# Attention by couples of heads or maps: three one-pass score products on 64-row tiles, A's values as fp32 on 64-column tiles

## The chip, the cores and the metric

The kernel runs on one NeuronCore of a Trainium2 chip. Its engines are named as in the profile: PE multiplies matrices (PEld is its loading of the stationary operand, the weights), DVE, ACT and POOL do vector work, SP issues the DMAs. The metric is the device time of one execution in microseconds (us), the median of a few runs.

## What is computed

One layer of an encoder for two groups of requests (prompt and sample), each with 1024 positions of 1024 channels, all in fp32. A common input projection feeds two attention branches. Branch A has 8 query heads and 2 key/value heads of 64 channels; branch B has 4 heads, each with two softmax maps of 64 channels, subtracted from each other, and values of 128 channels. Cut to what matters here:

```
# A: qa (S, 8, 64), ka and va (S, 2, 64), after RMSNorm and rotary positions; head j uses key/value head j // 4
s = einsum('bqgrd,bkgd->bgrqk', qblk, k) / sqrt(64)
p = softmax(s, axis=-1)
oa = einsum('bgrqk,bkgd->bqgrd', p, v) * silu(za)
# B: qb and kb (S, 4, 2, 64), vb (S, 4, 128)
s = einsum('bqhmd,bkhmd->bhmqk', qblk, k) / sqrt(64)
p = softmax(s, axis=-1)
pd = p[:, :, 0] - lam * p[:, :, 1]
ob = rms_norm(einsum('bhqk,bkhe->bqhe', pd, v), subln_g) * (1 - lam_init) * silu(zb)
# merge
merged = sigmoid(ga) * (oa @ w_proj_a) + sigmoid(gb) * (ob @ w_proj_b)
y = x + gate * (merged @ w_out)
```

## The kernel before

The two groups are worked on one after the other. A matrix product in full precision is made of one-pass products (type fp32r): each operand is split into a high part, the value rounded to fp32r, and a low part, the rest, and high x high, high x low and low x high are added in PSUM. The projections do that with three products for each block (`proj_tt` at L497 for 128 tokens x 256 columns, `z_gen` at L679, `merge_gen` at L950, `out_gen` at L979). An operand that stays plain fp32 needs no split; PE then takes more passes for one call.

**Scores.** A head has only 64 channels, and the array has 128 rows. `pairs_T` transposes q and k after the rotary step and stacks the high part of 64 channels on 64 partitions and the low part on the other 64: a head's [high; low] fills 128 rows. One product with [high; low] of q and of k gives high x high + low x low; for the cross terms `swapped` makes a copy of q with the halves exchanged, by four DMAs for each two query tiles of two maps (two for one head). So a tile of 128 queries x 1024 keys takes four products of 512 columns (L709, L710) into one score buffer `s` of two PSUM banks. There are two such buffers (`ps_s`).

**Softmax.** DVE takes the maximum of the tile (L711), ACT the exponential with the sum of a row (L712), into a buffer `p` (`ppool`, four of them). `flip` has DVE transpose 32 x 32 blocks in place (L745), for B after the two maps are combined (L744), and four DMAs bring the rows to their partitions in `pT` (L750, `qpool`, two buffers): the transposed weights of 256 queries.

**Values.** For A, `pT_pieces` splits `pT` into high and low in four pieces (ACT at L758, DVE at L759), and `a_values` multiplies a stationary operand that holds the high values of a head in 64 columns and the low ones in the other 64: for each of 8 blocks of keys one product with the high part (L770), one with the low part (L771). The result's two halves of 64 partitions are added at the end (L786, L787). For B the constant `WHOLE` makes the values plain fp32: one call for each block of keys, with 128 columns (L810).

**Order.** `units_of` lists the units of attention: A has 8 heads x 4 pairs of query tiles for each group, B 4 heads x 4. `attention` lays the steps of the units on a time axis: the scores of unit n at n and after, its values from n + `BEHIND`; a flip is issued after the next step. `weave` mixes these steps with the projections by fixed shares. All this only sets priorities: a scheduler with a timeline of its own then fixes the order on each engine, in which attention's steps go ahead (`tc.high_priority`). Engines work strictly in that order and wait for each other by semaphores. SP's queue holds every DMA of the kernel.

The functions concerned:

Of the kernel before, what the change touches and what calls it, by code (L numbers as in the profile page):

```python
# [20 lines left out]
P = 128  # L21
# [43 lines left out]
BEHIND = 1.4  # L65
AHEAD = 100
PV_LAG = 2

WHOLE = (True, True)
# [21 lines left out]
def kernel(ctx: ExitStack, tc: tile.TileContext, t: dict):  # L91
# [8 lines left out]
    qpool = ent(tc.tile_pool(name="qpool", bufs=2))  # L100
    tpool = ent(tc.tile_pool(name="tpool", bufs=2))
# [403 lines left out]
    def rms(ps, nh, e):  # L505
# [3 lines left out]
        nc.scalar.activation(raw, ps, AF.Copy)  # L509
# [31 lines left out]
    def pairs_T(x3, even, odd):  # L541


        nb = x3.shape[1] // 2
        ps = gbank()[:, : nb * P].rearrange("p (b n) -> p b n", b=nb)
        x = x3.rearrange("p (b two) d -> p b (two d)", two=2)
        for b in range(nb):
            nc.tensor.transpose(ps[:, b, :], x[:, b, :], ident)
        for dst, hi, lo in ((even, LO, HI), (odd, HI, LO)):
            nc.scalar.activation(dst[hi], ps[hi], AF.Copy)  # L550
            nc.vector.tensor_tensor(out=dst[lo], in0=ps[hi], in1=dst[hi].bitcast(F32), op=ALU.subtract)
# [15 lines left out]
    def swapped(u):  # L567

        qs = u["q"]
        sw = mtile("sw", [P, 2, 256], F32R)[:, : len(qs)]  # L570
        sl = slice(u["pr"] * 256, u["pr"] * 256 + 256)
        for m, q in enumerate(qs):
            for a, b in ((LO, HI), (HI, LO)):
                dma(sw[a, m].bitcast(F32), q[b, sl].bitcast(F32))
        return sw


    made = {}

# [3 lines left out]
    def kva_gen(ht, out):  # L583
        w = kva_w.pop()[0] if kva_w else load_w(w_cols(w_in, (C_KA, 256)))
        k = v2(utile())
        va = utile().rearrange("p (n k d) -> p n k d", n=NTT, k=2)
        out["ka"], out["va"] = k, va

        def front(tt, ps):
            e = by_turns(tt)  # L590
            x3, s3 = rms(ps[:, :128], 2, e)
            vp = ps[:, 128:256].rearrange("p (k d) -> p k d", k=2)
            vt = va[:, tt]
            nc.scalar.activation(vt[:, :, 0:64], vp, AF.Copy)
            nc.vector.tensor_tensor(out=vt[:, :, 64:128], in0=vp, in1=vt[:, :, 0:64].bitcast(F32), op=ALU.subtract)
            e.tensor_tensor(out=x3, in0=x3, in1=gka.unsqueeze(1).to_broadcast([P, 2, HD]), op=ALU.mult)
            rope(x3, s3, out["cosA"][:, tt], out["sinA"][:, tt], 16, e)
            return x3

        def back(tt, x3):  # L600
            sl = slice(tt * P, (tt + 1) * P)
            pairs_T(x3, k[:, 0:1, sl], k[:, 1:2, sl])
# [3 lines left out]
    def qa_gen(st, half):  # L606
        w = load_w(w_cols(w_in, (C_QA + half * 256, 256)))
# [4 lines left out]
        def front(tt, ps):  # L612
            e = by_turns(tt)
            x3, s3 = rms(ps, 4, e)
# [4 lines left out]
        def back(tt, x3):  # L619
            sl = slice(tt * P, (tt + 1) * P)  # L620
            pairs_T(x3, qs[0][:, :, sl], qs[1][:, :, sl])
            made[id(qs)] = tt + 1
# [3 lines left out]
    def qkb_gen(ht, out, h):  # L626
# [11 lines left out]
        def back(tt, x3):  # L638
            sl = slice(tt * P, (tt + 1) * P)
            pairs_T(x3, qk[0][:, :, sl], qk[1][:, :, sl])  # L640
            made[id(qk)] = tt + 1
# [3 lines left out]
    def vb_gen(ht, out, pr):  # L645
        w = load_w(w_cols(w_in, (C_VB + pr * 256, 256)))
        if WHOLE[pr]:
            v = utile().bitcast(F32).rearrange("p (n h e) -> p n h e", n=NTT, h=2)
            out[2 * pr], out[2 * pr + 1] = v[:, :, 0], v[:, :, 1]
        else:  # L650
            vs = [utile().rearrange("p (n s e) -> p n s e", n=NTT, s=2) for _ in range(2)]
            out[2 * pr], out[2 * pr + 1] = vs
        for tt in range(NTT):
            ps = yield from proj_tt(ht, w, tt)
            if WHOLE[pr]:
                nc.scalar.activation(v[:, tt].rearrange("p h e -> p (h e)"), ps, AF.Copy)
                yield 1
                continue
            for i in range(2):
                vp = ps[:, i * P : (i + 1) * P]  # L660
                nc.scalar.activation(vs[i][:, tt, 0, :], vp, AF.Copy)
                nc.vector.tensor_tensor(
                    out=vs[i][:, tt, 1, :], in0=vp, in1=vs[i][:, tt, 0, :].bitcast(F32), op=ALU.subtract
                )
# [38 lines left out]
    def softmax_unit(q, sw, k, pt, su):  # L703

        m = tiny.tile([P, 1], F32, tag="m", name=nm("m"))
        s = sbank()
        for n in range(2):
            sl = slice(n * 512, (n + 1) * 512)
            nc.tensor.matmul(s[:, sl], q, k[:, sl], start=True, stop=False)  # L709
            nc.tensor.matmul(s[:, sl], sw, k[:, sl], start=False, stop=True)  # L710
        nc.vector.tensor_reduce(out=m, in_=s, axis=AX.X, op=ALU.max, negate=True)  # L711
        nc.scalar.activation(  # L712
            pt.rearrange("p (j c a) -> p j c a", j=4, c=8), s.rearrange("p (c a j) -> p j c a", c=8, j=4),
            AF.Exp, bias=m, accum_out=su,
        )

    def scores(u, i):

        nm_ = len(u["q"])
        t, m = i // nm_, i % nm_  # L720
        qt = u["pr"] * 2 + t
        if "sw" not in u:
            u["sw"] = swapped(u)
        pt = ptile()
        su = u["su"][:, qt : qt + 1] if m == 0 else tiny.tile([P, 1], F32, tag="su", name=nm("su"))
        softmax_unit(u["q"][m][:, qt * P : (qt + 1) * P], u["sw"][:, m, t * P : (t + 1) * P], u["k"][m], pt, su)
        if m == 0:
            u[t] = [pt]
        else:
            f = tiny.tile([P, 1], F32, tag="r", name=nm("r"))  # L730
            nc.vector.reciprocal(f, su)
            nc.gpsimd.tensor_scalar(
                out=f, in0=f, scalar1=u["su"][:, qt : qt + 1], scalar2=nlam, op0=ALU.mult, op1=ALU.mult
            )
            u[t] += [pt, f]
        return t if m == nm_ - 1 else None

    def flip(u, t):


        pt = u[t][0]
        if len(u[t]) > 1:
            _, p1, f = u[t]
            nc.vector.scalar_tensor_tensor(out=pt, in0=p1, scalar=f, in1=pt, op0=ALU.mult, op1=ALU.add)  # L744
        nc.vector.transpose(pt, pt)  # L745
        if t == 0:
            u["pT"] = pair(F32R)
        dst = u["pT"].bitcast(F32).rearrange("p (i t f) -> p i t f", i=4, t=2)
        for i in range(4):
            dma(dst[:, i, t], pt[i * 32 : i * 32 + 32])  # L750

    def pT_pieces(u):

        pT = u["pT"].rearrange("p (q c b) -> p c q b", q=8, c=8)
        for cc in range(4):
            tl = pT[:, cc * 2 : cc * 2 + 2]
            th = tpool.tile([P, 2, 8, 32], F32R, tag="hi", name=nm("hi"), bufs=3)
            nc.scalar.activation(th, tl.bitcast(F32), AF.Copy)  # L758
            nc.vector.tensor_tensor(out=tl, in0=tl.bitcast(F32), in1=th.bitcast(F32), op=ALU.subtract)  # L759
            yield cc, th, tl  # L760

    def a_values(u):
        acc = ps_a.tile([P, 512], F32, tag="a", name=nm("a"))[:, :256]
        ready = []

        def pv(cc, th, tl):
            for c in range(2):
                k = cc * 2 + c
                lt = u["v"](k)
                nc.tensor.matmul(acc, lt, th[:, c, :], start=(k == 0), stop=False)  # L770
                nc.tensor.matmul(acc, lt, tl[:, c, :], start=False, stop=(k == 7))  # L771

        for piece in pT_pieces(u):
            ready.append(piece)
            if len(ready) > PV_LAG:
                pv(*ready.pop(0))
            yield 1
        while len(ready) > 1:
            pv(*ready.pop(0))
            yield 1  # L780
        pv(*ready.pop())
        tmp = mtile("at", [P, 256], bufs=1)
        o = mtile("oo", [P, 256])
        j = u["j"]
        a, b = (slice(0, 64), slice(64, 128)) if j % 2 == 0 else (slice(64, 128), slice(0, 64))
        nc.scalar.activation(tmp[a], acc[b], AF.Copy)  # L786
        nc.vector.tensor_tensor(  # L787
            out=query_order(o[a]), in0=piece_order(acc[a]), in1=piece_order(tmp[a]), op=ALU.add
        )
        pr = u["pr"]  # L790
        dma(u["od"][pr // 2][a, (pr % 2) * 256 : (pr % 2 + 1) * 256], o[a])
        yield 1

    def b_values(u):
        acc = ps_a.tile([P, 512], F32, tag="a", name=nm("a"))[:, :256]
        ready = []
        def pv(cc, th, tl):
            for c in range(2):
                k = cc * 2 + c
                for s, rt in ((0, th), (0, tl), (1, th)):  # L800
                    nc.tensor.matmul(
                        acc, u["v"][:, k, s, :], rt[:, c, :],
                        start=(k == 0 and s == 0 and rt is th), stop=(k == 7 and s == 1),
                    )

        if WHOLE[u["h"] // 2]:
            pT = u["pT"].bitcast(F32).rearrange("p (q c b) -> p c q b", q=8, c=8)
            yield 1
            for k in range(NCH):
                nc.tensor.matmul(acc, u["v"][:, k], pT[:, k], start=(k == 0), stop=(k == 7))  # L810
                if k % 2:
                    yield 1
        else:
            for piece in pT_pieces(u):
                ready.append(piece)
                if len(ready) > PV_LAG:
                    pv(*ready.pop(0))
                yield 1
            while len(ready) > 1:
                pv(*ready.pop(0))  # L820
# [361 lines left out]
```

## Time and profile before

| what | us |
|---|---|
| runs: median (lowest to highest) | 1984.13 (1981.57 to 1989.72) |
| span of the profiled execution | 1985.5 |
| DMA: mean rate over the span | 149 GB/s |
| mean granted TensorE clock | 0.982 of full |

The runs give the time of whole executions; the profile shows one of them instruction by instruction, and its span lies within 0.1% of the median. In the 40 equal slices of the span (49.6 us each) a digit is the busy share in tenths:

```profile
PE   8889999999999998999999899999999999999999
DVE  4558877777877577547465877677788845665641
ACT  4435655665654444754323565556655534566310
PEclk9899999999999999999999999999999999999999
```

PE is near full in every slice but the first; DVE and ACT have room on the mean, though not at every moment.

### The profile page before, as it was taken

Reading aid. Unit: us, or ns where it says so; the run is one execution under the profiler, and the core shown is the slowest. Engines: PE = TensorE matmul, PEld = TensorE weight load, DVE = VectorE, ACT = ScalarE, POOL = GpSimd, SP = SyncE. Lnnn points to the kernel's source line nnn. Section 1 sums busy time; section 2 is a strip of 40 time slices with the busy share of each in tenths; the row PEclk is TensorE's granted clock in tenths of the full one; section 3 lists DMA queues with packets and bytes.
Section 4 is the critical chain, followed back from the end, with each engine's and each line's share of the span. In section 5 each row is a group of like instructions: output and inputs, shape, how many; then the busy total and the mean of one; then the engine's idle time right before and its main releaser. Section 6 shows DMA issues by size and latency. Waiting matters only on the chain.

```text
span 1985.5 us, 30670 instructions
## 1 busy us (share of the span) xinstructions
PE 1908.6 (96%) x10466; PEld 1627.8 (82%) x10466; DVE 1330.8 (67%) x1906; ACT 1009.9 (51%) x1939; POOL 758.1 (38%) x1008
## 2 busy tenths in 40 slices
PE   8889999999999998999999899999999999999999
PEld 3878888888878994778888787888887888877887
DVE  4558877777877577547465877677788845665641
ACT  4435655665654444754323565556655534566310
POOL 2374612453446252221235464134445626422110
PEclk9899999999999999999999999999999999999999
DMA  8124556555553345865641455565654333567532
GB/s 310 33 80 126 155 152 169 152 166 154 133 153 102 101 120 173 257 227 167 222 149 35 140 144 145 149 164 144 184 137 137 106 97 99 156 212 245 174 101 75
DMA packets 269531, 295.11 MB, mean 149 GB/s; under 512 B 35776, under 2 KB 218176, under 8 KB 269376
## 3 DMA queue, kind: packets, MB, share of 16 engines
q1 hardware_dynamic: 269376, 293.15, 49.7%
q8 instruction: 84, 1.38, 0.3%
q14 instruction: 71, 0.58, 0.1%
HBM read 133.59 MB, written 42.01 MB: 88 GB/s over the span
## 4 chain that ended last, share of the span: by engine, by line
PE 68%; DMA 8%; DVE 8%; ACT 5%; SPq 4%; issue 3%; POOL 3%; ACTq 0%; POOLq 0%; DVEq 0%
PE f L497 16%; PE f L679 16%; PE f L950 6%; PE f L979 5%; PE s L709 4%; PE a L810 4%; PE s L710 4%; PE s L979 4%; DMA q<-p 3%; SPq L750 3%; PE s L950 2%; DVE q L759 2%; PE a L771 2%; PE a L770 2%; DVE m L711 2%
## 5 line engine op out<-in xcount | busy, mean ns | idle before, releaser
L679 PE MATMUL f<-u,w 128*128 128x512 f32 x2232 | 582.3, 398 | 0.1
L497 PE MATMUL f<-w,u 128*128 128x256 f32 x3456 | 487.0, 286 | 2.2 <-ACT ev L685 1.4
L497 PEld LDWEIGHTS f<-w,u 128*128 128x128 f32 x3456 | 459.5, 192 | 22.4 <-ACT ev L685 1.8
L679 PEld LDWEIGHTS f<-u,w 128*128 128x128 f32 x2232 | 408.8, 190 | 77.3 <-POOL w L181 0.8
L181 POOL TENSOR_TENSOR w<-st,w 128x512 fp32r<-128x512 f32 x168 | 230.3, 1390 | 439.9 <-ACT w L179 375.1
L712 ACT ACTIVATE p<-s,m 128x1024 f32<-128x1024 f32 x256 | 284.4, 1111 | 206.3 <-DVE m L711 111.3
L711 DVE TENSOR_REDUCE m<-s 128x1 f32<-128x1024 f32 x256 | 310.0, 1216 | 51.3 <-PE s L710 48.7
L745 DVE STREAM_TRANSPOSE p<-p 128x1024 f32<-128x1024 f32 x192 | 238.2, 1241 | 99.2 <-ACT p L712 86.5
L759 DVE TENSOR_TENSOR q<-q,hi 128x512 fp32r<-128x512 f32 x256 | 198.3, 792 | 60.6 <-ACT hi L758 58.6
L515 POOL TENSOR_TENSOR rs<-ss,nhalf 128x4 f32<-128x4 f32 (+1 forms) x112 | 112.8, 1007 | 322.8 <-DVE ss L514 284.0
L758 ACT ACTIVATE hi<-q 128x512 fp32r<-128x512 f32 x256 | 153.8, 625 | 104.1 <-DMA q<-p 55.4
L710 PE MATMUL s<-u,sw 128*128 128x512 f32 x512 | 206.7, 404 | 0.0
L179 ACT ACTIVATE w<-st 128x512 fp32r<-128x512 f32 x196 | 113.9, 625 | 97.2 <-DMA st<-in_w_in_dram 46.0
L950 PE MATMUL f<-u,w 128*128 128x512 f32 x552 | 133.4, 395 | 5.1 <-ACT ev L685 4.4
L770 PE MATMUL a<-hi,u 128*128 128x256 f32 x512 | 132.5, 285 | 2.1 <-DVE oo L787 2.1
L771 PE MATMUL a<-q,u 128*128 128x256 f32 x512 | 129.8, 286 | 1.2 <-DVE q L759 1.2
L810 PE MATMUL a<-q,u 128*128 128x256 f32 x512 | 128.3, 390 | 1.9 <-DVE oo L826 1.5
L950 PEld LDWEIGHTS f<-u,w 128*128 128x128 f32 x552 | 103.9, 190 | 27.2 <-ACT ev L685 4.7
L709 PE MATMUL s<-u 128*128 128x512 f32 x256 | 110.9, 433 | 15.1 <-ACT p L712 15.1
L810 PEld LDWEIGHTS a<-q,u 128*128 128x128 f32 x512 | 97.8, 196 | 17.5 <-DVE oo L826 1.6
L709 PE MATMUL s<-u,u 128*128 128x512 f32 x256 | 103.6, 405 | 8.3 <-ACT p L712 7.7
L710 PEld LDWEIGHTS s<-u,sw 128*128 128x128 f32 x512 | 98.4, 192 | 15.5
(175 smaller groups left out, 2562.1 us busy)
## 6 DMA issues: line engine op xcount, KB each, us to landing
q<-p SPq DMA_DIRECT2D x768, 128.0 KB, 2.6
st<-in_w_in_dram SPq DMA_DIRECT2D x132, 256.0 KB, 3.0
zd<-ev SPq DMA_DIRECT2D x96, 256.0 KB, 2.2
sw<-u SPq DMA_DIRECT2D x256, 64.0 KB, 2.1
p<-zd SPq DMA_DIRECT2D x64, 256.0 KB, 3.2
u<-in_w_ada_dram SPq DMA_DIRECT2D x8, 1024.0 KB, 10.4
st<-in_w_in_dram SPq DMA_DIRECT2D x64, 128.0 KB, 2.7
st<-in_w_out_dram SPq DMA_DIRECT2D x32, 256.0 KB, 2.9
```

The source lines that it names most:

```text
L181: e.tensor_tensor(out=wl, in0=st, in1=wh.bitcast(F32), op=ALU.subtract)
L497: nc.tensor.matmul(ps, lt[c][:, sl], w[:, c, wi, :], start=(k == 0), stop=(k == 23))
L679: nc.tensor.matmul(ps, w[:, c, wi, e * P : (e + 1) * P], rt[c], start=(k == 0), stop=(k == 23),)
L709: nc.tensor.matmul(s[:, sl], q, k[:, sl], start=True, stop=False)
L710: nc.tensor.matmul(s[:, sl], sw, k[:, sl], start=False, stop=True)
L711: nc.vector.tensor_reduce(out=m, in_=s, axis=AX.X, op=ALU.max, negate=True)
L712: nc.scalar.activation(pt.rearrange("p (j c a) -> p j c a", j=4, c=8), s.rearrange("p (c a j) -> p j c a", c=8, j=4), AF.Exp, bias=m, accu ...
L745: nc.vector.transpose(pt, pt)
L759: nc.vector.tensor_tensor(out=tl, in0=tl.bitcast(F32), in1=th.bitcast(F32), op=ALU.subtract)
L810: nc.tensor.matmul(acc, u["v"][:, k], pT[:, k], start=(k == 0), stop=(k == 7))
L950: nc.tensor.matmul(ps, w[:, c, wi, d * P : (d + 1) * P], o[:, oi, :], start=(k == 0), stop=(k == 11))
L979: nc.tensor.matmul(ps, w[:, c, wi, e * P : (e + 1) * P], m[:, mi, :], start=(k == 0), stop=(k == 23))
```

## The change

Attention works on **couples**: for A the heads j and j + 4, which use different key/value heads; for B the two maps of a head.

- **q and k.** `split_T` replaces `pairs_T`: the transposed tile of two heads (128 partitions, 64 for each) is split into a high tile and a low tile, by one ACT and one DVE instruction on 128 partitions instead of two each on 64. `swapped` and its DMAs go. `qa_gen` loads two pieces of 128 columns so that a couple's heads lie together, and `rms` crosses them (`crossed=True`).
- **Scores.** `scores` makes a group for one query tile of a couple: for each half of the keys and each of the three terms high x high, low x high, high x low (`TERMS`) one product for each of the two heads. Each product uses 64 rows of the array, one head the lower 64, the other the upper 64, and the heads alternate: 12 products of 512 columns. Low x low is no longer computed. The group takes both score buffers, and its first product is made to wait for the exponentials of the group before.
- **Values of A.** No split: `va` and `pT` are plain fp32. A unit is a couple, and each call of `a_values` uses 64 columns of the array and writes 64 partitions of the accumulator; the heads alternate: 16 calls of 256 columns. One ACT instruction copies the result. `qpool` has three buffers, and a unit of A takes two.
- **Order.** `together` binds a group: its first product is placed by the scheduler as before, each following one is tied behind the one before it and gets the highest priority. A's units are half as many, each with two steps of scores and two of values (`PAIRS`).
- B's values stay as they are. The shares of the projections in `weave` are unchanged.

The diff, cut to its core:

```diff
+PAIRS = (1.3, 0.3)
+TERMS = ((0, 0), (1, 0), (0, 1))
+TOP = 100000
 AHEAD = 100
-PV_LAG = 2
-WHOLE = (True, True)
...
-    qpool = ent(tc.tile_pool(name="qpool", bufs=2))
-    tpool = ent(tc.tile_pool(name="tpool", bufs=2))
+    qpool = ent(tc.tile_pool(name="qpool", bufs=3))
...
-    def pairs_T(x3, even, odd):
+    def split_T(x3, hi, lo):
...
-        for dst, hi, lo in ((even, LO, HI), (odd, HI, LO)):
-            nc.scalar.activation(dst[hi], ps[hi], AF.Copy)
-            nc.vector.tensor_tensor(out=dst[lo], in0=ps[hi], in1=dst[hi].bitcast(F32), op=ALU.subtract)
+        nc.scalar.activation(hi, ps, AF.Copy)
+        nc.vector.tensor_tensor(out=lo, in0=ps, in1=hi.bitcast(F32), op=ALU.subtract)
+    def together(calls, after=()):
+        prev = None
+        for call in calls:
+            if prev is None:
+                ins = call()
+                for other in after:
+                    behind(ins, other, mybir.DependencyClass.Sync)
+            else:
+                with tc.high_priority(offset=TOP):
+                    ins = call()
+                behind(ins, prev, mybir.DependencyClass.NoSync)
+            prev = ins
...
-            nc.tensor.matmul(s[:, sl], q, k[:, sl], start=True, stop=False)
-            nc.tensor.matmul(s[:, sl], sw, k[:, sl], start=False, stop=True)
...
+        ss = [sbank(), sbank()]
+        for n in range(2):
             sl = slice(n * 512, (n + 1) * 512)
+            for i, (a, b) in enumerate(TERMS):
+                for m in (1, 0):
+                    rows = (LO, HI)[m]
+                    calls.append(lambda m=m, a=a, b=b, rows=rows, sl=sl, i=i: nc.tensor.matmul(
+                        ss[m][:, sl], u["q"][a][rows, qs], u["k"][b][rows, sl],
+                        start=(i == 0), stop=(i == len(TERMS) - 1),
+                    ))
+        together(calls, list(exps))
...
     def a_values(u):
         acc = ps_a.tile([P, 512], F32, tag="a", name=nm("a"))[:, :256]
...
+        together([
+            lambda k=k, m=m: nc.tensor.matmul(
+                acc[(LO, HI)[m]], u["v"][:, k, m], pT[m][:, k], start=(k == 0), stop=(k == 7)
+            )
+            for k in range(NCH) for m in (1, 0)
+        ])
+        yield 1
         o = mtile("oo", [P, 256])
+        nc.scalar.activation(query_order(o), piece_order(acc), AF.Copy)
...
-            na, nv = (2, 4 + PV_LAG) if ph < 2 else (4, 5 + PV_LAG)
-            steps += [(n + i / na, ph, n, i, True) for i in range(na)]
-            steps += [(n + BEHIND + i / nv, ph, n, i, False) for i in range(nv)]
+            nv, behind, pace = (2, *PAIRS) if ph < 2 else (7, BEHIND, 1.0)
+            steps += [(n + i / 2, ph, n, i, True) for i in range(2)]
+            steps += [(n + behind + i * pace / nv, ph, n, i, False) for i in range(nv)]
```

How the instructions move is seen in the order in which each engine holds them. On PE, in the first half of A's heads of the first request group, before (`s` is a score buffer, `u` q, k or a part of the input, `sw` the swapped q, `f` a projection's bank, `w` its weights, `a` the accumulator of A's values, `hi` and `q` the two parts of the transposed weights):

```order
L497 MATMUL f_1868<-w_1435,u_283 128x256
L497 MATMUL f_1868<-w_1435,u_284 128x256
L497 MATMUL f_1868<-w_1435,u_283 128x256 x2
L497 MATMUL f_1868<-w_1435,u_284 128x256
L771 MATMUL a_1682<-q_1573,u_397 128x256
L770 MATMUL a_1682<-hi_1730,u_397 128x256
L771 MATMUL a_1682<-q_1573,u_397 128x256
L497 MATMUL f_1868<-w_1435,u_327 128x256 x2
L709 MATMUL s_1956<-u_396,u_927 128x512
L710 MATMUL s_1956<-u_396,sw_1888 128x512
L709 MATMUL s_1956<-u_396,u_927 128x512
L710 MATMUL s_1956<-u_396,sw_1888 128x512
```

The same place now, at the end of one group of scores, with the values of a couple after it and before the next group:

```order
L714 MATMUL s_1925<-u_393,u_904 128x512
L714 MATMUL s_1924<-u_393,u_904 128x512
L668 MATMUL f_2084<-u_324,w_1865 128x512
L668 MATMUL f_2084<-u_325,w_1865 128x512
L668 MATMUL f_2084<-u_324,w_1865 128x512
L496 MATMUL f_2190<-w_1396,u_530 128x256 x2
L496 MATMUL f_2190<-w_1396,u_531 128x256
L496 MATMUL f_2190<-w_1396,u_530 128x256 x2
L496 MATMUL f_2190<-w_1396,u_531 128x256
L496 MATMUL f_2190<-w_1396,u_530 128x256 x2
L496 MATMUL f_2190<-w_1396,u_531 128x256
```

```order
L496 MATMUL f_2190<-w_1396,u_548 128x256
L753 MATMUL a_1974<-q_1805,u_394 64x256
L753 MATMUL a_1974<-q_1804,u_394 64x256
L753 MATMUL a_1974<-q_1805,u_394 64x256
L753 MATMUL a_1974<-q_1804,u_394 64x256
L753 MATMUL a_1974<-q_1805,u_394 64x256
```

Where products of scores and values stood alone among the projections, they stand in closed groups: 12 of scores (122 of the 128 groups exactly so, one more run holds nearly two of them), 16 of values (all 32). Over the whole program PE goes 133 times into a run of scores, 32 times into a run of A's values and 147 times back to other work.

On DVE, in the same phase, before (L711 the maximum, L745 the transposition, L759 the low part of a piece, L787 the addition of the halves):

```order
L711 TENSOR_REDUCE m_2737<-s_2738 128x1
L745 STREAM_TRANSPOSE p_2695<-p_2695 128x1024
L759 TENSOR_TENSOR q_2429<-q_2429,hi_2600 128x2x8x32
L787 TENSOR_TENSOR oo_2575<-a_2465,at_2574 64x4x2x32
L711 TENSOR_REDUCE m_2782<-s_2783 128x1
L745 STREAM_TRANSPOSE p_2736<-p_2736 128x1024
L759 TENSOR_TENSOR q_2429<-q_2429,hi_2625 128x2x8x32
L759 TENSOR_TENSOR q_2552<-q_2552,hi_2692 128x2x8x32
```

and now:

```order
L695 TENSOR_REDUCE m_1908<-s_1892 128x1
L695 TENSOR_REDUCE m_1911<-s_1893 128x1
L744 STREAM_TRANSPOSE p_1906<-p_1906 128x1024
L744 STREAM_TRANSPOSE p_1907<-p_1907 128x1024
L517 TENSOR_REDUCE ss_2135<-row_2132 128x4
L553 TENSOR_TENSOR u_1418<-f_2147,u_1417 128x2x128
L518 TENSOR_SCALAR ss_2135<-ss_2135 128x4
L695 TENSOR_REDUCE m_1940<-s_1924 128x1
L695 TENSOR_REDUCE m_1943<-s_1925 128x1
```

The maxima of a couple and its transpositions now come in twos, and the instructions on pieces are gone.

224 lines of the change are left out of this document (75 added, 149 removed).

## The prediction

> **What bounds the kernel now.** I read the page's engine shares first, then its chain, then the groups, then PE's waits, and last the timeline, to get from instruction to instruction.
>
> ```profile
> PE 1908.6 (96%) x10466; PEld 1627.8 (82%) x10466; DVE 1330.8 (67%) x1906; ACT 1009.9 (51%) x1939; POOL 758.1 (38%) x1008
> PE 68%; DMA 8%; DVE 8%; ACT 5%; SPq 4%; issue 3%; POOL 3%; ACTq 0%; POOLq 0%; DVEq 0%
> ```
>
> PE is idle for 1985.5 - 1908.6 = 76.9 us only, and two thirds of the chain is its own work. So the change is worth what it does to PE's time, and the other engines matter as far as PE waits for them. What PE waits for (waiting line, releaser, us in total, times, longest):
>
> ```profile
> PE s L709 <- ACT p L712: 22.8, 20, 4.0
> PE a L770 <- DVE oo L787: 2.1, 1, 2.1
> PE a L771 <- DVE q L759: 1.2, 2, 0.9
> ```
>
> The groups that the change touches (count | busy us, mean ns of one | idle before):
>
> ```profile
> L709 PE MATMUL s<-u 128*128 128x512 f32 x256 | 110.9, 433 | 15.1 <-ACT p L712 15.1
> L710 PE MATMUL s<-u,sw 128*128 128x512 f32 x512 | 206.7, 404 | 0.0
> L770 PE MATMUL a<-hi,u 128*128 128x256 f32 x512 | 132.5, 285 | 2.1 <-DVE oo L787 2.1
> L771 PE MATMUL a<-q,u 128*128 128x256 f32 x512 | 129.8, 286 | 1.2 <-DVE q L759 1.2
> L759 DVE TENSOR_TENSOR q<-q,hi 128x512 fp32r<-128x512 f32 x256 | 198.3, 792 | 60.6 <-ACT hi L758 58.6
> L758 ACT ACTIVATE hi<-q 128x512 fp32r<-128x512 f32 x256 | 153.8, 625 | 104.1 <-DMA q<-p 55.4
> ```
>
> A mean of 404 ns is not what a product costs, since products overlap; the distance from start to start is. The timeline (start us, us, engine, line):
>
> ```profile
> 508.49 0.28 PE L770 MATMUL a<-hi,u 128*128 128x256 f32 x1
> ...
> 509.80 0.28 PE L771 MATMUL a<-q,u 128*128 128x256 f32 x1
> 509.92 0.29 PE L497 MATMUL f<-w,u 128*128 128x256 f32 x1
> ...
> 512.46 0.40 PE L709 MATMUL s<-u 128*128 128x512 f32 x1
> 512.70 0.39 PE L710 MATMUL s<-u,sw 128*128 128x512 f32 x1
> 512.92 0.40 PE L709 MATMUL s<-u 128*128 128x512 f32 x1
> 513.16 0.39 PE L710 MATMUL s<-u,sw 128*128 128x512 f32 x1
> 513.39 1.07 PE L679 MATMUL f<-u,w 128*128 128x512 f32 x4
> ...
> 568.60 1.46 PE L810 MATMUL a<-q,u 128*128 128x256 f32 x6
> ```
>
> The four score products take 513.39 - 512.46 = 0.93, so **0.231 us** each (512 columns, one pass). The twelve value products ahead of it take 509.92 - 508.49 = 1.43, so **0.119 us** each (256 columns, one pass). An fp32 product of 256 columns is recorded twice (512 records for 256 calls at L810): six records, (1.46 - 0.38) / 5 = **0.216 us** a record, 0.43 a call.
>
> **What is removed.** Scores: 256 tiles x 4 products x 0.231 = 236.5 us. A's values: 64 units x 16 x 0.119 = 121.9. And the first load of a tile is often exposed: L709's mean of 433 against 404 for L710 is 0.029 x 256 = 7.4, call it 8. Together 366 us of PE. Off PE: the splits of the transposed weights (L758, L759), the adding of halves for A, half the instructions of the q/k splits, 256 DMAs for the swapped q.
>
> **What is added on PE, if pairs overlap.** The trace has no two tiles of the array at work together, so the overlap itself is bounded: from two at the price of one (a slot of 0.231 holds both) to none. I take the first: a pair uses different rows or columns of the array and writes different banks, or different partitions of one, and the nearest rows show that PE runs independent work side by side (a load beside a product at 755.55, quoted below). Scores: 128 groups x 6 slots x 0.231 = 177.4. Values: 32 groups of 16 fp32 calls, 32 records; the second record of one map runs beside the first of the other, so 17 slots x 0.216 = 3.67, x 32 = 117.5. Sum 295, which is 71 below what goes.
>
> **What a change of tile shape costs.** This is what eats the 71. The trace has a few such changes, around the products with only two columns of weights (L435):
>
> ```profile
> 753.84 1.45 PE L435 MATMUL f<-st,cT 128*2 128x512 f32 x3
> 755.22 0.19 PEld L709 LDWEIGHTS s<-u 128*128 128x128 f32 x1 [0.86 <-DVE u L551]
> 755.22 0.50 PE L709 MATMUL s<-u 128*128 128x512 f32 x1
> 755.33 0.19 PEld L710 LDWEIGHTS s<-u,sw 128*128 128x128 f32 x1
> 755.55 0.40 PE L710 MATMUL s<-u,sw 128*128 128x512 f32 x1
> 755.56 0.65 PEld L832 LDWEIGHTS f<-ones_c,at 128*128 128x128 f32 x4
> ...
> 773.38 0.40 PE L710 MATMUL s<-u,sw 128*128 128x512 f32 x1
> 773.71 0.59 PE L435 MATMUL f<-st,cT 128*2 128x512 f32 x1
> ```
>
> Into the narrow shape, at 773: from L710 to L435 0.33 instead of 0.23, so 0.10. Out of it, at 755: the three L435 stand (1.45 - 0.59) / 2 = 0.43 apart, the third starts at 754.70, L709 at 755.22: 0.52, so 0.09 more. And the next load is no longer hidden: PEld L709 starts with its product, not a product earlier, and L709 to L710 takes 0.33, again 0.10 more. The loads follow each other at 755.22 and 755.33: a load of 128 columns occupies its path for 0.107.
>
> So, by the order of the changed program, which changes shape 312 times:
> - 133 entries into the 64-row shape: 0.10 + 0.107 for the first load, + 0.107 until the other half is loaded = 0.31; 41 us.
> - 32 entries into the 64-column shape: 0.10 + 0.05 (half the columns); 5 us.
> - 147 returns to the whole array: 0.09 + 0.10; 28 us.
>
> 74 in all; the rows bound it from 0 (each change falls where PE waits anyway) to 74. I take it whole, since PE rarely waits. Products and changes: 295 + 74 - 366 = **+3 us**. The new products are worth nothing by themselves.
>
> **What is won off PE.** The splits were 198.3 of DVE's 1330.8 and 153.8 of ACT's 1009.9: 15% of each, and some smaller pieces go with them. PE's 76.9 us of idle time lie partly in the first 140 us, which the change hardly touches:
>
> ```profile
> 0.00:60.00 60.00, 52.34 (x192) 25.82 (x193) 26.40 (x48) 24.46 (x41) 12.57 (x16) 0.89 0.79 274
> 60.00:140.00 80.00, 69.52 (x468) 64.29 (x467) 50.93 (x130) 36.01 (x98) 43.81 (x62) 0.95 0.14 44
> ```
>
> 7.7 + 10.5 = 18 there (the second number is the stretch, the third PE busy), 59 after. Bounds: nothing, to some 45 of them. I take a quarter, 15: the waits for L787 and L759 vanish and the one for L712 shrinks. On SP's queue the 256 swap DMAs go and 16 weight loads come (q's columns in two pieces). One wait stays there:
>
> ```profile
> SPq L750 <- PE a L771: 88.1, 40, 6.1
> ```
>
> A's transposed weights wait for the values of the unit before to free their buffer, and the weight loads queue behind. With three buffers and two taken by a unit it waits as before; PE's projections, whose weights lie a tile ahead, hide it, and uncovered it could cost its 88 at most.
>
> Sum against the profiled execution: 1985.5 + 3 - 15 = 1973.5; that execution lies 1.4 above the median of the runs, so **1972 us**.
>
> **The new wait.** A group takes both score banks, so its first product waits for both exponentials of the group before. Queued behind it are the projections on PE, whose banks ACT and DVE wait for. The softmax of a group:
>
> ```profile
> L711 DVE TENSOR_REDUCE m<-s 128x1 f32<-128x1024 f32 x256 | 310.0, 1216 | 51.3 <-PE s L710 48.7
> L712 ACT ACTIVATE p<-s,m 128x1024 f32<-128x1024 f32 x256 | 284.4, 1111 | 206.3 <-DVE m L711 111.3
> ...
> 515.00 1.23 DVE L711 TENSOR_REDUCE m<-s 128x1 f32<-128x1024 f32 x1
> 520.47 1.12 ACT L712 ACTIVATE p<-s,m 128x1024 f32<-128x1024 f32 x1 [0.89 <-DMA q<-p]
> ...
> busy tenths in 40 slices 0002222212232223200000222222123321230000
> ```
>
> With free engines that is 2 x 1.22 + 1.11 = 3.5, and some tenths for the last drain. PE's other work between groups: exponentials run in 28 of the 40 slices of 49.6 us (last row), 1390 / 128 = 10.9 a group, less 1.9 for the group, 9.0 (by the order and the rows above half the gaps are under 7.6). So 3.5 fits well; but the tile of 512.46 ended at 513.55 and its exponential at 521.59, 8.0 later, through queues. I cost the wait at nothing beyond today's 22.8, because those queues held the splits.
>
> **The rivals.**
> - **Half a pair.** The load of a 64-row tile cannot run while the product in the same rows does. For it speaks that an exposed load is just what the changes of shape show; against it that within one shape loads run beside products (755.56 above). A slot is then 0.231 + 0.107; 768 x 0.107 = +82: about **2054**. The Trainium skill states it so (TensorE: Matmul & The Clock Gate, part 3, The mechanism): a weight load overlaps a running matmul only when the row groups differ; the whole-array rows here do not agree. By the speedups measured on that page for four row tiles, 3.07, the estimate would be a slot of 0.30 and some 2025.
> - **No pair at all**, the change does not do what it says: values alone +15 slots x 0.216 x 32 = +104, **2076**; scores too, +177, **2253**. Nothing in the trace speaks for or against.
> - **The bank wait decides** (slower). If queues stay as at 512, a group's chain is 8.0 + 2.3 for the second reduction and exponential = 10.3, over 9.0 by 1.3: in the 64 groups of A +83, **2055**. It decides once the chain passes the work between groups. For it: SP and the weight tiles still hold exponentials up (the row of 520.47 waits for a DMA). Against: DVE and ACT lose 15% or more.
> - **More relief** (faster): idle falls by 45, and the second half's load runs beside the first's (-14): **1928**.
>
> **How the numbers follow.** The forecast, with its own range 1950 to 1995, 0.48; half a pair 0.12; no pair 0.12; bank wait 0.13; relief 0.15. What lies within 0.5% (1974 to 1994) a measurement of this kernel cannot tell from no change. Faster: 0.25 of the forecast's 0.48, and relief's 0.15: 0.40. Same: 0.18. Slower: 0.05 of the forecast's, and 0.37 of the three rivals: 0.42. The range leaves out "no pair" and the ends of the others: 1915 to 2070.
>
> **What would show it.** In the profile after: the two products of a pair start within about 0.11 and the next pair 0.23 later (0.34: half a pair; every product 0.23 after the last: none). The first whole-array product behind a group has its load start with it. PE's waits have a row of the scores for L695's and L698's work, its total near 20 (over 60: the bank wait). DVE falls under 1130 busy and ACT under 860. I am wrong if PE's own time, without waits, moves by over 20 us either way.

## The result, and the profile after

The changed kernel takes 2004.47 us (median of 4 runs, 2002.37 to 2009.5) against 1984.2 before: a ratio of 1.0109, 95% interval 1.0083 to 1.0135. The forecast was 1972. The time lies in the stated range, but on the other side of the kernel before. The profile below shows the slowest of the four runs (2009.5).

The page of the changed kernel: span, engine shares, and PE's and the clock's digits over 40 slices.

```profile
span 2007.7 us, 30209 instructions
PE 1900.4 (95%) x10978; PEld 1525.8 (76%) x10978; DVE 1052.5 (52%) x1458; ACT 819.8 (41%) x1547; POOL 710.8 (35%) x1008
PE   8889999999998998799999899999999899987999
PEclk9899999999999999899999899999999999988999
PE 73%; DMA 8%; DVE 5%; ACT 4%; issue 4%; POOL 3%; SPq 3%; ACTq 0%; POOLq 0%; DVEq 0%
```

DVE lost 278 us of work and ACT 190, PE 8 of busy time. But PE's idle time rose, from 76.9 to 107.3, and the clock falls below full in more slices.

One group of scores in the timeline of PE, with the loads (PEld) beside it:

```profile
501.27 1.08 PE L668 MATMUL f<-u,w 128*128 128x512 f32 x4
502.28 0.50 PE L714 MATMUL s<-u 64*128 64x512 f32 x2
502.62 0.62 PE L714 MATMUL s<-u,u 64*128 64x512 f32 x4
503.08 0.40 PE L714 MATMUL s<-u 64*128 64x512 f32 x2
503.31 0.63 PE L714 MATMUL s<-u,u 64*128 64x512 f32 x4
503.87 0.50 PE L496 MATMUL f<-w,u 128*128 128x256 f32 x2
...
502.28 0.18 PEld L714 LDWEIGHTS s<-u 64*128 64x128 f32 x2 [0.36 <-issue]
502.39 0.42 PEld L714 LDWEIGHTS s<-u,u 64*128 64x128 f32 x4
503.87 0.42 PEld L496 LDWEIGHTS f<-w,u 128*128 128x128 f32 x3 [0.36 <-issue]
```

Two products stand under 502.28 and last 0.50 together: the pair starts at once. The next pair comes 0.34 later, its first load not being hidden; from 502.62 to 503.08 two pairs take 0.46, so a slot is 0.23. The loads come in twos as well: two of 128 columns under 502.28 and the next at 502.39. The last L668 starts at 501.27 + 3 x 0.23 = 501.96, so entering costs 0.32 - 0.23 = 0.09; the first product behind the group again has its load with it. From 502.28 to 503.87 are 1.59, with 0.09 ahead and 0.10 for the load behind **1.78** a group, against 8 x 0.231 = 1.85 for the two tiles before. A group of A's values, and the row of all of them:

```profile
1308.92 3.87 PE L753 MATMUL a<-q,u 128*64 128x256 f32 x32 [0.94 <-DMA q<-p]
1312.72 0.72 PE L668 MATMUL f<-u,w 128*128 128x512 f32 x2
...
L753 PE MATMUL a<-q,u 128*64 128x256 f32 x1024 | 119.6, 385 | 4.8 <-DMA zd<-ev 3.1
```

1312.72 - 1308.92 = 3.80 with its changes of shape, against 32 x 0.119 = 3.81 before. So PE's work itself fell a little: 128 x 0.07 = 9 us.

**Where the time is lost.** I cut both executions at the first score and the last value of each stretch, and in each took from its length the work of PE: products counted, times their cost from rows such as these (0.227, 0.120, 0.216 for an fp32 record, 0.231 for a score before; 1.78 and 3.81 for the new groups with their changes of shape). The rest is waiting and clock.

| stretch | before: us, above the work | after: us, above the work |
|---|---|---|
| start, to the first score | 149.4, 35.5 | 146.3, 32.4 |
| first request group: A | 363.1, 6.7 | 345.1, 3.3 |
| B, first three heads | 229.2, 11.4 | 245.5, 14.0 |
| **B, last head** | **102.4, 16.6** | **124.3, 37.1** |
| to the second group's first score | 259.9, 10.0 | 252.8, 7.9 |
| second group: A | 361.8, 16.3 | 318.5, 17.3 |
| B, first three heads | 235.7, 17.8 | 282.1, 15.3 |
| **B, last head** | **110.4, 13.8** | **115.4, 30.0** |
| tail | 173.6, 4.2 | 177.7, 5.5 |
| sum | 1985.5, 132.3 | 2007.7, 162.8 |

The lengths of A and of B's first three heads differ mostly because projections moved from one to the other; what lies above the work did not. The sum above the work rose by 30.5, and the last heads alone by 20.5 + 16.2 = 36.7. The work fell by 8.3. In windows over the last heads (stretch, then busy of PE, PEld, DVE, ACT, POOL, granted clock, DMA share, GB/s), before and after:

```profile
742.00:844.00 102.00, 92.79 (x386) 63.97 (x385) 65.91 (x92) 64.91 (x99) 26.46 (x34) 0.97 0.69 215
1701.00:1812.00 111.00, 101.90 (x452) 83.78 (x451) 72.58 (x96) 69.99 (x106) 28.92 (x34) 0.97 0.67 212
```

```profile
737.00:861.00 124.00, 99.92 (x419) 65.99 (x419) 70.64 (x94) 74.71 (x108) 28.22 (x38) 0.90 0.71 213
1715.00:1830.00 115.00, 94.96 (x428) 73.17 (x425) 66.74 (x87) 75.77 (x108) 22.46 (x24) 0.88 0.66 203
```

PE idles 24 and 20 us there instead of 9 and 9, and the clock is at 0.90 and 0.88 instead of 0.97. What happens in between is seen in the timeline of the second one:

```profile
1771.59 1.10 ACT L696 ACTIVATE p<-s,m 128x1024 f32<-128x1024 f32 x1
1773.32 0.50 PE L714 MATMUL s<-u 64*128 64x512 f32 x2
1774.34 0.64 PE L714 MATMUL s<-u,u 64*128 64x512 f32 x4
1777.75 1.28 ACT L853 ACT_TABLE_LOAD   x1 [4.45 <-DMA row<-zd]
1779.71 0.69 DVE L858 TENSOR_TENSOR row<-row,row 128x512 f32<-128x512 f32 x1 [3.21 <-ACT row L853]
1780.00 1.01 PE L784 MATMUL f<-ones_c,at 128*128 128x1 f32 x4 [3.66 <-ACT at L777]
1782.43 2.35 DVE L695 TENSOR_REDUCE m<-s 128x1 f32<-128x1024 f32 x2
1783.68 1.11 ACT L696 ACTIVATE p<-s,m 128x1024 f32<-128x1024 f32 x1
1784.91 1.28 ACT L853 ACT_TABLE_LOAD   x1
1786.20 0.63 ACT L853 ACTIVATE row<-row 128x512 f32<-128x512 f32 x1
1786.85 1.28 ACT L696 ACT_TABLE_LOAD   x1
1788.14 1.11 ACT L696 ACTIVATE p<-s,m 128x1024 f32<-128x1024 f32 x1
1790.29 0.50 PE L714 MATMUL s<-u 64*128 64x512 f32 x2
```

The group ends at 1774.98. Its maxima (L695) stand on DVE behind gating (L858), which waits for ACT (L853), which waits for a DMA: 7.4 us. Between the two exponentials (L696) ACT then runs a SiLU of the gating (L853), and loads a table of 1.28 us before it and another after it: 3.4 us from the end of the first to the start of the second. The second ends at 1789.25, and only then, at 1790.29, does the next group run: 17 us from group to group. The group waits for both exponentials, so nothing of the next query tile can be done ahead.

The gating shows in ACT's work as well. ACT has 190 us less to do in the whole program, but in the two windows it is busy 150.5 us against 134.9 before, and the stretches of the last heads hold 21 and 20 table loads against 15 and 15. The splits of A that were taken away never stood there.

PE's waits over the whole program do not name the chain:

```profile
PE a L772 <- DMA row<-zd: 12.3, 2, 10.4
PE s L714 <- ACT p L696: 12.2, 5, 8.2
PE f L784 <- ACT at L777: 8.7, 4, 3.7
PE a L772 <- DMA q<-p: 7.0, 4, 2.6
```

The wait at the scores is shorter than before (22.8). In the second of the last heads the late chain is booked on what comes after it: B's values (L772: 10.4 of the 12.3) and the sums of squares (L784). In the first one the longest waits stand at weights, 5.6 us at L434 for a DMA and 5.4 us at L898 for ACT; whether they too hang on the chain is not shown.

### The profile page after: what moved, and what is told of

The parts are those of the page before. It is cut to its first block, busy times and chain, and to the rows that moved or that the text cites. A ratio compares the mean times of both kernels' runs of the same rounds, so it can differ in the third digit from the quotient of the medians.

```text
span 2007.7 us, 30209 instructions
## 1 busy us (share of the span) xinstructions
PE 1900.4 (95%) x10978; PEld 1525.8 (76%) x10978; DVE 1052.5 (52%) x1458; ACT 819.8 (41%) x1547; POOL 710.8 (35%) x1008
## 4 chain that ended last, share of the span: by engine, by line
PE 73%; DMA 8%; DVE 5%; ACT 4%; issue 4%; POOL 3%; SPq 3%; ACTq 0%; POOLq 0%; DVEq 0%
PE f L668 21%; PE f L496 17%; PE s L714 8%; PE a L753 6%; PE f L898 6%; PE f L927 4%; PE a L772 4%; PE s L927 2%; PE s L898 2%; SPq L747 2%; DMA q<-p 2%; DMA st<-in_w_in_dram 1%; DMA row<-zd 1%; ACT p L696 1%; POOL w L180 1%
## 5 line engine op out<-in xcount | busy, mean ns | idle before, releaser
L668 PE MATMUL f<-u,w 128*128 128x512 f32 x2232 | 577.7, 403 | 0.5 <-ACT ev L674 0.5
L668 PEld LDWEIGHTS f<-u,w 128*128 128x128 f32 x2232 | 408.3, 191 | 98.0 <-issue 19.6
L496 PEld LDWEIGHTS f<-w,u 128*128 128x128 f32 x3456 | 445.3, 192 | 39.2 <-issue 20.3
L695 DVE TENSOR_REDUCE m<-s 128x1 f32<-128x1024 f32 x256 | 301.0, 1217 | 289.3 <-PE s L714 288.8
L696 ACT ACTIVATE p<-s,m 128x1024 f32<-128x1024 f32 x256 | 285.1, 1115 | 274.8 <-DVE m L695 248.3
L714 PE MATMUL s<-u,u 64*128 64x512 f32 x1280 | 189.6, 405 | 9.4 <-ACT p L696 9.4
L772 PE MATMUL a<-q,u 128*128 128x256 f32 x512 | 137.2, 416 | 34.1 <-DMA row<-zd 12.3
L714 PEld LDWEIGHTS s<-u,u 64*128 64x128 f32 x1280 | 117.2, 186 | 48.6 <-issue 13.8
L772 PEld LDWEIGHTS a<-q,u 128*128 128x128 f32 x512 | 103.3, 210 | 55.6 <-issue 17.4
L898 PE MATMUL f<-u,w 128*128 128x512 f32 x552 | 132.6, 395 | 1.9 <-DVE u L909 1.9
L753 PE MATMUL a<-q,u 128*64 128x256 f32 x1024 | 119.6, 385 | 4.8 <-DMA zd<-ev 3.1
L898 PEld LDWEIGHTS f<-u,w 128*128 128x128 f32 x552 | 104.0, 190 | 23.8 <-DVE u L909 2.3
L753 PEld LDWEIGHTS a<-q,u 128*64 128x64 f32 x1024 | 73.8, 138 | 44.2 <-issue 6.8
L927 PE MATMUL f<-u,w 128*128 128x512 f32 x456 | 105.6, 389 | 0.0
L730 POOL TENSOR_SCALAR r<-r,suB,nlam 128x1 f32<-128x1 f32 x64 | 22.6, 354 | 232.3 <-DVE r L729 231.8
L739 DVE SCALAR_TENSOR_TENSOR p<-p,r,p 128x1024 f32<-128x1024 f32 x64 | 84.6, 1321 | 29.4 <-POOL r L730 27.0
L927 PEld LDWEIGHTS f<-u,w 128*128 128x128 f32 x456 | 85.6, 188 | 17.8
## 6 DMA issues: line engine op xcount, KB each, us to landing
u<-in_w_ada_dram SPq DMA_DIRECT2D x8, 1024.0 KB, 10.4
```

What stands on the lines that cost most here:

```text
L496: nc.tensor.matmul(ps, lt[c][:, sl], w[:, c, wi, :], start=(k == 0), stop=(k == 23))
L668: nc.tensor.matmul(ps, w[:, c, wi, e * P : (e + 1) * P], rt[c], start=(k == 0), stop=(k == 23),)
L696: exps.append(nc.scalar.activation(pt.rearrange("p (j c a) -> p j c a", j=4, c=8), s.rearrange("p (c a j) -> p j c a", c=8, j=4), AF.Exp, ...
L714: calls.append(lambda m=m, a=a, b=b, rows=rows, sl=sl, i=i: nc.tensor.matmul(ss[m][:, sl], u["q"][a][rows, qs], u["k"][b][rows, sl], start ...
L753: lambda k=k, m=m: nc.tensor.matmul(acc[(LO, HI)[m]], u["v"][:, k, m], pT[m][:, k], start=(k == 0), stop=(k == 7))
L898: nc.tensor.matmul(ps, w[:, c, wi, d * P : (d + 1) * P], o[:, oi, :], start=(k == 0), stop=(k == 11))
```

## The experiments

All are edits of the changed kernel. Ratios are to the kernel before, on the same chip as the run, with the 95% interval; there the kernel before took 1979.7 to 1981.8.

**e1, the mixture of the last head.**

```diff
-LAST_ATT, LAST_FILL = (48, 28)
+LAST_ATT, LAST_FILL = (39, 28)
```

> One constant: LAST_ATT 48 to 39, the count of attention steps by which the last head is mixed with other work (its steps went from 44 to 36 with the change, the constant stayed). Theory A (the last head's mixture is stale: its products come too early against the other work): the two stretches of the last head, 124 and 115 us in the changed kernel, each fall by 5 to 15, time 1980 to 1995. Theory B (the mixture as a whole lacks work that can cover the last head, whatever its order): within 5 of 2004. Theory C (changes of tile shape carry the loss): no change, within 5 of 2004.

1992.65, ratio 1.0065 (1.0044 to 1.0085). Some 9 us better, but not where expected: the last heads take 131 and 118 us, with 7 to 9 us more work in each and 36.5 and 24.3 above it; the rest of the gain is spread over the program. Theory A is not supported.

**e2, no wait for both exponentials.**

```diff
-        together(calls, list(exps))
+        together(calls)
```

> The first product of a group no longer waits for the exponentials of the group before (each score bank still waits for its own). By the order the first product then goes ahead alone in 80 groups, and PE changes tile shape 462 times instead of 312. Theory D (waiting for both banks makes the last head's chain long): the last head's stretches fall by 10 or more each, elsewhere 150 changes x 0.2 = 30 us come on top: 2005 to 2020. Theories A and B: the stretches stay as they are, and the changes of shape cost 20 to 35: 2025 to 2040.

2042.37, ratio 1.0300 (1.0268 to 1.0332), 38 us above the changed kernel; last heads 123 and 123. The loss is a little more than the 20 to 35 us expected for the extra changes of shape. For theory D it proves little: the second product of a group still needs the other bank, so the group as a whole starts no sooner.

**e3, more cover in the last head.**

```diff
-    (7, 20, 5, 3, 2, 5),
-    (7, 18, 4, 2, 5, 6),
+    (7, 15, 5, 3, 2, 5),
+    (7, 13, 4, 2, 5, 6),
-LAST_ATT, LAST_FILL = (48, 28)
+LAST_ATT, LAST_FILL = (48, 43)
```

> Five of the 48 shares of the z projections of each request group move from the second half of A to the last head of B (Z_SHARE 20 to 15 and 18 to 13, LAST_FILL 28 to 43): 120 products of 0.227 us, 27 us of work each. Theory B (the last head lacks cover): the work above what PE's products need, 37 and 30 us in the two stretches of the last head, falls by about half, time 1970 to 1985. Theory A or D: the stretches grow by the 27 us that they are given and A shrinks by as much, within 6 of 2004.

1983.22, ratio 1.0015 (1.0002 to 1.0028). Above the work the last heads have 22.5 and 19.5 us left, from 37.1 and 30.0: a good third less, not half. The time lies at the upper edge of theory B's range. The theory itself is not shown by this run: of the 120 products moved for each request group only 32 and 61 ran within the last heads, whose work grew by 1 and 16 us. In the first one some 14 us were won with hardly any more cover, while ACT's table loads there fell from 21 to 12.

**e4, groups not bound.**

```diff
-                with tc.high_priority(offset=TOP):
-                    ins = call()
-                behind(ins, prev, mybir.DependencyClass.NoSync)
+                ins = call()
```

> Groups are not bound: only the first product's place is kept as it is, the others are placed by the scheduler like any other product. PE changes shape 726 times instead of 312, and 163 score products stand alone, without a partner. If a change costs 0.19 to 0.20 us as the rows show (0.09 to enter or leave, 0.10 for a load that is not hidden): 414 x 0.195 = 81 us, and some 80 lost half slots of 0.115 = 9: 2080 to 2100. If changes of shape are mostly hidden: under 2030.

2172.59, ratio 1.0965 (1.0941 to 1.0989): 168 us above the changed kernel, twice what was expected. A place where score products and projections alternate shows both halves of it:

```profile
535.05 0.50 PE L712 MATMUL s<-u 64*128 64x512 f32 x1
535.48 0.51 PE L666 MATMUL f<-u,w 128*128 128x512 f32 x1
535.91 0.49 PE L712 MATMUL s<-u 64*128 64x512 f32 x1
...
542.24 0.79 PE L712 MATMUL s<-u 64*128 64x512 f32 x1
542.96 0.58 PE L496 MATMUL f<-w,u 128*128 128x256 f32 x1
543.47 0.79 PE L712 MATMUL s<-u,u 64*128 64x512 f32 x1
...
538.70:552.40 13.70, 13.70 (x28) 6.55 (x27) 2.36 (x2) 1.21 (x2) 1.61 (x6) 0.50 0.00 0
```

At first a product takes 0.43 from start to start, 0.23 and 0.20 for the change of shape, as in the sum of the prediction. From 538.7 the clock is granted at half (last row, of the windows), though PE is not idle for a moment, and a score product takes 0.72. The mean clock of the run is 0.947, against 0.973. By the mean clocks, an estimate, that costs 0.053 x 2171.9 - 0.027 x 2007.7 = 61 us, beside the 90 that were expected.

**e5, the maps of the last head apart.**

```diff
-        together(calls, list(exps))
+        if u.get("h") == 3:
+            for m in (0, 1):
+                together(calls[1 - m :: 2])
+        else:
+            together(calls, list(exps))
```

> Only in the last head of B the products of the two maps are no longer alternated: six for map 0, then six for map 1, each six bound by itself and waiting for its own score bank alone. No two products overlap there, so 16 groups need 48 slots x 0.231 = 11 us more of PE per request group... of which the last heads are 2 x 8 groups x 6 slots = 22 us in all. Theory D (serial chain: both banks at once, so scores of a query tile start only after both exponentials of the tile before): the last head's stretches, 124 and 115 us, fall by 5 to 15 in spite of it; time 1980 to 2000. If the chain of two banks is not what makes the last head long: the stretches grow by up to 11 each, 2010 to 2025.

1988.07, ratio 1.0042 (1.0025 to 1.0059). The last heads take 98 and 101 us, though their products cost more, since no two overlap:

```profile
730.00:828.00 98.00, 88.76 (x358) 58.15 (x357) 60.00 (x85) 53.88 (x82) 23.90 (x35) 0.97 0.62 184
1699.00:1801.00 102.00, 99.30 (x421) 75.81 (x419) 64.14 (x82) 66.08 (x99) 21.07 (x24) 0.93 0.68 209
```

PE idles 9 and 3 us in them, from 24 and 20. Theory D's forecast holds, beyond its range in one of the two stretches (27 and 14 us shorter). But the edit takes away more than that the two maps hold both banks together, since everything else is placed anew with it: the two stretches hold 28 table loads instead of 41, and the first has 95 products of the z projections instead of 144.

**e6, gating later.**

```diff
-GATED_A = -0.2
+GATED_A = -0.6
```

> GATED_A -0.2 to -0.6: the gating of the other heads (SiLU on ACT with its table loads, products on DVE that wait for loads of z) is mixed in later in the last head. Theory G (the reductions and exponentials of the last head queue on DVE and ACT behind gating that waits for its loads, 4 to 7 us a tile): the last head's stretches fall by 10 or more each, part of it comes back after them as uncovered gating; 1985 to 2000. If gating is not in the way: 2000 to 2015.

1994.49, ratio 1.0060 (1.0035 to 1.0085). The last heads shrink to 97 and 104 us; the stretches behind them idle 19 and 10 us, from 5 and 5, with the gating that now has no cover. Theory G's forecast holds. The groups still take both banks here, and yet PE idles only 9 and 11 us in the last heads; 15 table loads are left in them, from 41.

**e7 to e10, together.** e7 is e3 with LAST_ATT 39; e8 moves three shares more (Z_SHARE 12 and 10, LAST_FILL 52); e9 is e5 with e3; e10 is e5 with LAST_ATT 39.

> e1 and e3 together: LAST_ATT 39, LAST_FILL 43, five shares more of z in the last head. If the two act on the same lack of cover, no better than e3: 1980 to 1985. If they act apart: 9 + 18 us below the changed kernel's ratio of 1.011, so 0.996 to 0.999 of before, 1972 to 1978 on this chip.

> As e7 with eight shares moved instead of five (Z_SHARE 12 and 10, LAST_FILL 52). Theory B: the work above PE's products in the last heads falls further, some 5 to 8 us in all below e7. If A's second half now lacks cover itself, the time there rises and the sum is e7's or above.

> e5 and e3 together: the last head's maps apart, and five shares more of z in it. Theory D with B (the last head is a serial chain that lacks cover): each took 16 to 25 us off what lies above PE's products, the two overlap in the last head, so the sum gives 0.993 to 0.999 of before, 1967 to 1979 on this chip. If both remove the same waits: as e3, 1983.

> e5 with LAST_ATT 39. Theory D: the mixture of the last head no longer matters much once its chain is short, within 5 of e5 (1988). Theory A: another 5 to 10 below e5.

| run | us | ratio (95%) | above the work, all stretches |
|---|---|---|---|
| changed kernel | 2004.47 | 1.0109 (1.0083 to 1.0135) | 162.8 |
| e3 | 1983.22 | 1.0015 (1.0002 to 1.0028) | 135.2 |
| e7 | 1985.97 | 1.0017 (1.0000 to 1.0035) | 136.2 |
| e8 | 2003.26 | 1.0111 (1.0078 to 1.0144) | 151.7 |
| e9 | 1985.52 | 1.0015 (0.9999 to 1.0031) | 137.1 |
| e10 | 1987.65 | 1.0034 (1.0018 to 1.0050) | 145.2 |

The gains do not add: e7 is no better than e3, nor is e9. I had hoped for 0.993 to 0.999 from e9 and was wrong. For e9 and e10 the last column holds some 22 us of PE's own work, since it counts a group of the last heads at 1.78 although its products no longer overlap (16 groups x 6 x 0.231). PE idles 9 and 6 us in e9's last heads against 16 and 11 in e3's: the edit of e5 did remove waits beyond e3, and the lost overlap cost at least what that brought. e8 gives everything back: its last heads have 38 and 43 us more work than the changed kernel's and 32 and 25 us above it, so more work alone is no cover.

**e11, only the values of A taken back.** `pT` is split into pieces by ACT and DVE again, and each head of a couple takes 16 one-pass products of 128 columns:

```diff
+            for cc in range(4):
+                tl = pT[:, cc * 2 : cc * 2 + 2]
+                th = tpool.tile([P, 2, 8, 32], F32R, tag="hi", name=nm("hi"), bufs=2)
+                nc.scalar.activation(th, tl.bitcast(F32), AF.Copy)
+                nc.vector.tensor_tensor(out=tl, in0=tl.bitcast(F32), in1=th.bitcast(F32), op=ALU.subtract)
...
+                    nc.tensor.matmul(acc, u["v"][:, k, m], th[:, c, :], start=(k == 0), stop=False)
+                    nc.tensor.matmul(acc, u["v"][:, k, m], tl[:, c, :], start=False, stop=(k == 7))
```

> Only the values of A are taken back: the transposed weights are split into high and low parts on ACT and DVE again, 32 one-pass products of 128 columns for a couple instead of 32 fp32 records on 64 columns; the scores stay as changed. PE's own time: 32 x 0.119 = 3.81 against 3.81 for a group of values with its changes of shape, no difference. DVE gets 225 us and ACT 178 back. If relief of DVE and ACT is worth time (my prediction's 15 us): 2015 to 2030. If PE hardly waited for the splits: 2000 to 2008.

2054.40, ratio 1.0371 (1.0348 to 1.0395): 50 us worse than the changed kernel, more than either theory said.

```profile
L763 PE MATMUL a<-hi,u 128*128 128x256 f32 x512 | 137.5, 292 | 27.4 <-DVE oo L779 16.4 <-DMA q<-p 7.3 <-ACT hi L769 3.6
```

PE waits 27 us at these products (2.1 in the kernel before): 16.4 for DVE's addition of the halves of an earlier result (L779), 7.3 for DMAs and only 3.6 for ACT's part of the split. What the run loses lies in A and B's first heads; the last heads have 35 and 31 us above the work, as with the fp32 values. So the last heads' loss does not come from the values of A. The run is no pure undoing: it has two buffers for the pieces, not three, a lead of one piece, not two, and the two heads of a couple share one bank of the accumulator. How much of the 50 us belongs to the splits and how much to these is not shown.

**e12, more cover and gating later.** e3 with GATED_A -0.4.

> e3 (five shares more of z in the last head) with the gating mixed in later there (GATED_A -0.4). Theory: cover and gating act on the same serial chain; with the added work as cover, gating that comes later no longer stands ahead of the reductions and still finds work beside it: 0.994 to 1.000 of before. If e3 has already hidden what gating delays: as e3, 1.000 to 1.003.

1975.12, ratio **0.9973** (0.9957 to 0.9989): the one version that is faster than the kernel before, by 0.3%. The last heads idle 14 and 7 us at a clock of 0.97, and the sum above the work is 127.3.

```profile
705.00:811.00 106.00, 92.40 (x416) 62.94 (x415) 53.89 (x74) 43.60 (x74) 23.03 (x34) 0.97 0.59 177
1666.00:1776.00 110.00, 103.08 (x486) 81.05 (x483) 60.53 (x75) 56.66 (x90) 21.27 (x24) 0.97 0.57 174
```

**A rival that no run tests by itself: ACT's table loads.** An ACT_TABLE_LOAD takes 1.28 us, and the traces show one where ACT goes from exponentials to the functions of the gating and the merge (L853, L889) or back. The two last heads hold 30 of them before, 41 in the changed kernel, 45 in e1, 39 in e2 and 41 in e11, which leave the loss there as it was, but 28 in e3 and e5 and 15 in e6 and e12, which lessen it. The count alone does not decide, since e7 and e8 have 34 and 28 and PE still idles 35 and 38 us there. No edit changes the count and nothing else.

A third score buffer, which would loosen the chain without giving up the pairs, was not tried.

## Why the prediction was right or wrong

- **Pairs overlap: right.** The slot is 0.23, as taken. "Half a pair" and "no pair" fell. The rule of the Trainium skill that was weighed there (TensorE: Matmul & The Clock Gate, part 3) is not what these rows show: the loads at 502.39 run while the products of 502.28 are in the same rows. The speedup of 3.07 for four row tiles, from the same page of the Trainium skill, is 77% of four, and the two tiles here reach all of two: two products in 0.23, where one takes 0.231.
- **Changes of shape: right, one piece too dear.** 0.09 and 0.10, as read off L435. The 0.107 for the second half's load is not paid, since both halves load at once: 133 x 0.107 = 14 us. Values were put at 3.67 and changes of shape on top; 3.80 holds both. So PE's own work came out at -8 instead of +3. (The +3 also took 8 us off for exposed loads before, which the costs of the table leave out; against +11 the two pieces, 14 and some 7, are nearly the whole difference.)
- **"What is won off PE": this step failed.** I took 15 us of PE's idle time away on the ground that DVE and ACT have less to do. They had 278 and 190 us less, and idle time rose by 30.4. 1985.5 - 8.3 + 30.5 gives the 2007.7 of the profiled execution; 30.5 holds the idle time, the lower clock that follows it, and small gains elsewhere. The waits that I named did go or shrink, but the time came back at other products. The relief also fell in the wrong place: no split of A stands in the last heads, where DVE is busy 137 us against 138 before and ACT 150 against 135. Less work for an engine is not less waiting when the chain through it gets longer.
- **"The new wait", costed at nothing: the same error seen from its place.** The ground given was that the queues had held the splits; in the last head they hold gating. And the chain of a group was put against the mean work between groups, 9.0 us. In the last heads the groups follow each other at 10 to 17 us once gating stands in the same queues, and the work between groups must be found there, not on the mean. With the maps apart (e5) or gating later (e6) PE idles there 12 and 21 us in sum instead of 44, against 18 before. As far as these two runs can be read, the loss needs both: groups that wait for two exponentials, and gating that stands ahead of them.
- **The rival "the bank wait decides"** had the mechanism, but in the 64 groups of A, with 83 us. A lost nothing (23.0 us above the work before and 20.6 after, in sum); B's last heads lost 37. And the sign that I named for it, PE's row for scores behind the exponentials, fell from 22.8 to 12.2.
- **"More relief"** fell as a whole. e11 hints that relief was there, since with the splits back the same scores cost 50 us more, but it differs in more than the splits.
- What remains open: how the loss of a last head divides between the held banks, the order of DVE's and ACT's queues and ACT's table loads. Each edit reorders everything (e10's two last heads take 119 and 105 us, e5's 98 and 101), so single stretches can be read to some 15 us only.

## What to carry to other kernels

Two 64-row products side by side cost one, but each change of tile shape costs 0.2 us of PE, so groups must be long and closed: here PE's work fell by 8 us, where the overlap alone was counted at 71. When two buffers that took turns are taken together, ask what can still run ahead, and ask it in the stretch where other work stands in the same queues, not on the mean. After such a change the shares and the order by which other work is mixed into that stretch have to be set anew; by the ratios that brought 27 us here (e12).

## What the runs showed that I had not expected

- **The clock falls with PE busy.** In e4, 13.7 us without a gap in PE, but with a change of shape at each product, were granted half the clock, and the same alternation had run at full clock for some 3.6 us before. The run has twelve such stretches, 113 us together. In the other kernels here the half clock follows stretches in which PE waits, but for those between 43 and 61 us, which follow products of one column (L273 before, L272 now). A change of shape so costs twice: 0.2 us, and with many in a row the clock.
- **Both halves of the array load at once.** Two loads of 128 columns in 0.107 us (502.28 to 502.39), where the whole array takes 0.107 for one.
